# An inner seven-product scheme for one product of the SwiGLU up stage, from the third pair of column tiles on

## The chip, the cores and the metric

The kernel runs on one core of one Trainium2 chip. The metric is the device time of one execution in microseconds (us), the median of several runs; below, a time is that of the whole kernel unless a stage is named. The engines are TensorE (PE, with its weight loads shown apart as PEld), VectorE (DVE), ScalarE (ACT), GpSimd (POOL) and SyncE (SP, which here only issues DMAs).

## What is computed

One block of an encoder on a sequence of 1024 tokens with 1024 channels, in float32. The part that matters here is the last one: the norm and the SwiGLU feed-forward network with 2816 hidden columns.

```python
mod = (silu(c) @ w_ada + b_ada)
shift1, scale1, gate1, shift2, scale2, gate2 = split(mod, 6)
h = rms_norm(x, norm1_w) * (1 + scale1) + shift1
x = x + gate1 * hybrid_mixer(h, w_in, ..., w_out)   # gated DeltaNet heads beside a short gated conv
h = rms_norm(x, norm2_w) * (1 + scale2) + shift2
x = x + gate2 * ((silu(h @ w_gate) * (h @ w_up)) @ w_down)
return rms_norm(x, norm_f_w)
```

## The kernel before, in words

**Arithmetic.** Large products are made in a rounded float32 format (fp32r) from split operands: each operand is a high part (rounded, made by ACT) and a low part (the rest, made by DVE), and a product is three matmuls, high x high, high x low and low x high, added in one PSUM bank. A matmul has a 128 x 128 stationary operand and a moving one of 512 columns; a bank holds 128 x 512.

**Stages.** The conditioning vector and the w_in projection come first, then the two head groups, w_out, the norm, the up stage (gate and up) and the down stage. Until the w_out stage a planner sets the order of the instructions; its lines show as L448 in the profile. From the second half of w_out on, the order is written out by hand, and each engine's instructions show as L89 (PE) or L90 (the others), the lines of the helper that issues them.

**The w_out stage, second half.** `w_out_tile(t, ch)` is one tile of 128 tokens by 512 channels; `norm_tile` and `norm_stats` make the norm of a token tile (ACT sums the squares, POOL works on one column, DVE scales). `first_half` transposes the first four normed token tiles into operand tiles `H[k][0]` for eight groups k of 128 channels: k = 0 to 3 are the operand B11, k = 4 to 7 are B21. `tr_split` is four transposes into a bank, then the high part on ACT and the low part on DVE. `sums_x(i)` makes the operand sums of the outer scheme, in place; `early_load` and `early_mat` get the first weights ready.

**The up stage.** It runs over 11 pairs p = 0 to 10 of column tiles (256 of the 2816 hidden columns, for gate and up, q = 0 and 1). In each pair the two halves of the channels and the two halves of the tokens form a 2 x 2 block product, made with seven block products in place of eight (the scheme of Strassen and Winograd). The list `STEPS` names their order, the bank and the operands of each:

```python
STEPS = (("X", "A11", "B11", True), ("Y", "A12", "B21", True), ("X", "S2", "T2", False), ("Z", "S1", "T1", True),
         ("X", "S3", "T3", False), ("Z", "S4", "B22", False), ("X", "A22", "T4", False))
```

A operands are weights and their sums S1 to S4 (they change with each pair: class `Weights` with `load`, `sum_n`, `cast` for the high part on ACT, `low` on DVE). B operands are tokens and their sums T1 to T4; they are fixed, made once in pair 0. `run(p, s)` issues step s of pair p on PE: two q of four k of three matmuls, 24 in all, each of 512 columns. `block(p, s)` follows it and issues what the other engines do behind that step: `keep` (ACT copies a bank into SBUF), `close` (DVE adds a bank to such a copy), `silu`, `act` (the product of the gate and up halves), the weights of later steps, and DMA writes of finished results (`store`, issued by `flush` on SP). `block(p, 6)` makes the weights A12 of the next pair's step 1; `block(p, 0)` makes the sums S1 and S2 and the last product of the pair before, `c[o]["z5"][1]`. `slot` hands out the SBUF tiles for split weights from a ring of eight; `prep_load`, `prep_gate` and `prep_sums` make operand sums of w_down for the down stage. Pair 0 has an order of its own, since its steps wait for the fixed operands (`t_split` makes T2, T1, T3, T4 and B22 there, each with four banks of transposes).

The order of the instructions on each engine is the order in which the program issues them. A tile's pool and its tag decide which buffer it takes, and an instruction waits until the last user of that buffer is done.

Of the kernel before, what the change touches and what calls it, by code (L numbers as in the profile page):

```python
# [51 lines left out]
def kernel(  # L52
# [79 lines left out]
    def flat(ap):  # L132
        return ap.rearrange("p a b -> p (a b)")
# [69 lines left out]
    def h_slot(k, hf):  # L203
        return hp_.tile([P, 2, HT], F32R, name=nm(f"h{k}_{hf}"), tag=f"H{k}_{hf}")
# [337 lines left out]
    s2c = cst.tile([P, KB], F32, name="s2c", tag="s2c")  # L542
    b2c = cst.tile([P, KB], F32, name="b2c", tag="b2c")
    db2 = cst.tile([P, 4], F32, name="db2", tag="db2")
    su = []

    sim = Sim(seq, dict(pe=T_START[0], dve=T_START[1], act=T_START[2], pool=T_START[3], sp=T_START[4]))
# [952 lines left out]
    def pmm(o, l, r, s_, e_, more=False):  # L1500
        pe("pe", PE.matmul(o, l, r, start=s_, stop=e_, skip_group_check=more))
# [36 lines left out]
    def norm_tile(t):  # L1538
        keep_x2(t, (0,))
        norm_scale(t, norm_stats(t))  # L1540
# [25 lines left out]
    def first_half(ks):  # L1566
        for k in ks:
            H[k][0] = tr_split(lambda: h_slot(k, 0), [x2n[i][:, k * P:(k + 1) * P] for i in range(4)], allb.get("tr"), b2c[:, k:k + 1])

    def w_out_tile(t, ch):  # L1570
# [40 lines left out]
    first_half(range(4))  # L1611
    w_out_tile(5, 1)
    keep_x2(5, (1,))
    first_half(range(4, 8))
    early_load(0)
    early_load(1)
    sums_x(0)
    w_out_tile(5, 0)
    norm_tile(5)
    w_out_tile(6, 1)  # L1620
    keep_x2(6, (1,))
    sums_x(1)
    w_out_tile(6, 0)
    norm_tile(6)
    w_out_tile(7, 1)
    early_mat(0)
    norm_stats(7, 1)
    sums_x(2)
    early_mat(1)
# [13 lines left out]
    class Weights:  # L1643
# [53 lines left out]
        def mat(self, n):  # L1697
            for q in range(2):
                self.cast(n, q)
                self.low(n, q)  # L1700

    n_slot = [0]

    def slot():
        n_slot[0] += 1
        n = n_slot[0] - 14
        if n <= 0 or n % 8 in (5, 6, 7, 0):
            return hl_t([P, 2, 4, P])
        return mp.tile([P, 2, 4, P], F32R, name=nm("u"), tag="gl", bufs=4)
# [24 lines left out]
    def run(p, s, q_=(0, 1)):  # L1734
        b, an, bn, first = STEPS[s]
        if first and 0 in q_:
            for q in (0, 1):
                bk[p][q][b] = bank_tile(bk[p][q][b], "acc")
        for q in q_:
            u, ps = W[p].u[an][q], bk[p][q][b]  # L1740
            for k in range(4):
                x_ = B[bn][k]
                for n, (wi, xi) in enumerate(((0, 0), (0, 1), (1, 0))):
                    pmm(ps, u[:, wi, k, :], x_[:, xi, :], first and k == 0 and n == 0, k == 3 and n == 2, not first)

    def cc(p, n):
        if p == 0 and n == "p1":
# [27 lines left out]
    def store(p, n, t):  # L1775
        pend.append((am_scr[p, A_IX[n]], t))
# [28 lines left out]
    def block(p, s):  # L1805
        w, n = W.get(p), W.get(p + 1)
        last = p == NP - 1
        if s == 0:
            if p > 0:
                o = p - 1  # L1810
                ACT.activation(c[o]["z5"][1], bk[o][0]["X"], AF.Silu)
            if w:
                w.sum_n("S1")
                w.sum_n("S2")
                for q in (0, 1):
                    w.cast("S2", q)
            if p > 0:
                a12 = c[o]["z5"][1]
                DVE.tensor_tensor(a12, bk[o][1]["X"], a12, ALU.mult)
                store(o, "A12", a12)  # L1820
            if w:
                for q in (0, 1):
                    w.low("S2", q)
        elif s == 1:
            if w:
                keep(p, "p1", "X")
                w.cast("S1", 0)
                w.cast("S1", 1)
            if p > 0:
                o = p - 1  # L1830
                a11, s1, a21 = c[o]["p1"][0], c[o]["p1"][1], c[o]["u2"][0]
                DVE.tensor_tensor(a11, s1, a11, ALU.subtract)
                DVE.tensor_tensor(a21, c[o]["z5"][1], a11, ALU.subtract)
                store(o, "S2", a11)
                store(o, "S4", a21)
            if w:
                w.low("S1", 0)
                w.low("S1", 1)
                w.sum_n("S3")
        elif s == 2:  # L1840
            close(p, "p1", "Y")
            w.cast("S3", 0)
            silu(p, "p1")
            w.cast("S3", 1)
            w.low("S3", 0)
            w.low("S3", 1)
            act(p, "p1")
            store(p, "A11", c[p]["p1"][0])
            w.sum_n("S4")
        elif s == 3:  # L1850
            keep(p, "u2", "X")
            w.mat("S4")
            prep_gate(p - 1)
        elif s == 4:
            keep(p, "z5", "Z")
            w.mat("A22")
            prep_sums(p - 1)
            if last:
                first_mats(0, "A11", am_scr)
        elif s == 5:  # L1860
            close(p, "z5", "X")
            if n:
                n.cast("A11", 0)
            silu(p, "z5")
            if n:
                n.cast("A11", 1)
                n.low("A11", 0)
                n.low("A11", 1)
            act(p, "z5")
            store(p, "A22", c[p]["z5"][0])  # L1870
            if last:
                first_mats(1, "B11", None)
        elif s == 6:
            close(p, "u2", "Z")
            if n:
                n.cast("A12", 0)
            silu(p, "u2")
            if n:
                n.cast("A12", 1)
                n.low("A12", 0)  # L1880
                n.low("A12", 1)
            act(p, "u2")
            a11, a21, a22, s1, s3 = c[p]["p1"][0], c[p]["u2"][0], c[p]["z5"][0], c[p]["p1"][1], c[p]["u2"][1]
            DVE.tensor_tensor(s1, a21, a22, ALU.add)
            DVE.tensor_tensor(s3, a11, a21, ALU.subtract)
            store(p, "S1", s1)
            store(p, "S3", s3)
            if last:
                first_mats(2, "A12", am_scr)

# [80 lines left out]
    for p in range(1, NP):  # L1971
        for s in range(7):
            if s == 0:
                prep_load(p - 1)
            if s == 3 and p < NP - 1:
                W[p + 1] = Weights(p + 1)
                W[p + 1].load(0)
            if s == 5 and p < NP - 1:
                W[p + 1].load(1)
            if p == NP - 1 and s in (3, 5, 6):  # L1980
                first_load(*{3: (0, "A11"), 5: (1, "B11"), 6: (2, "A12")}[s])
            if s != 6:
# [217 lines left out]
```

## Time and profile before

| | us |
|---|---|
| median of 3 runs | 1166.29 (1165.78 to 1166.97) |
| profiled execution, its own time | 1166.65 |
| its span, first to last instruction | 1164.9 |
| PE busy | 1154.4 (99%) |
| DVE busy | 921.1 (79%) |
| ACT busy | 542.7 (47%) |
| POOL busy | 61.9 (5%) |

The granted TensorE clock is 0.999 of full speed. Busy time of an engine is the time that its own records cover. The records of PE are longer than their spacing, since matmuls are pipelined: what a matmul costs in a full queue is the distance between the starts of two of them, not the length of its record. In the timeline, a row is a run of like instructions with the start of the first and the length of all; the bracket at its end is the idle time of the engine ahead of it and what ended it.

### The profile page before, as it was taken

Reading aid. Unit: us, or ns where it says so; the run is one execution under the profiler, and the core shown is the slowest. Engines: PE = TensorE matmul, PEld = TensorE weight load, DVE = VectorE, ACT = ScalarE, POOL = GpSimd, SP = SyncE. Lnnn points to the kernel's source line nnn. Section 1 sums busy time; section 2 is a strip of 40 time slices with the busy share of each in tenths; the row PEclk is TensorE's granted clock in tenths of the full one; section 3 lists DMA queues with packets and bytes.
Section 4 is the critical chain, followed back from the end, with each engine's and each line's share of the span. In section 5 each row is a group of like instructions: output and inputs, shape, how many; then the busy total and the mean of one; then the engine's idle time right before and its main releaser. Section 6 shows DMA issues by size and latency. Waiting matters only on the chain.

```text
span 1164.9 us, 16388 instructions
## 1 busy us (share of the span) xinstructions
PE 1154.4 (99%) x5552; PEld 965.7 (83%) x5552; DVE 921.1 (79%) x1702; ACT 542.7 (47%) x1181; POOL 61.9 (5%) x100
## 2 busy tenths in 40 slices
PE   9999999999999999999999999999999999999997
PEld 7888888888888888888888888888888888888886
DVE  7899889899987898658776777776777687688676
ACT  6779633469634552326333333333333365443343
POOL 1110001002101010200000000000000000000002
PEclk9999999999999999999999999999999999999999
DMA  9823454534225455434164466445554589869403
GB/s 358 325 91 102 150 163 147 187 112 154 89 77 161 160 193 194 163 107 147 61 235 145 139 217 205 165 143 208 190 192 141 183 328 394 293 204 340 144 33 145
DMA packets 127540, 209.15 MB, mean 180 GB/s; under 512 B 20576, under 2 KB 45152, under 8 KB 127456
## 3 DMA queue, kind: packets, MB, share of 16 engines
q1 hardware_dynamic: 122080, 204.90, 51.3%
q10 hardware_dynamic: 5376, 3.21, 0.9%
q8 instruction: 44, 0.72, 0.2%
q14 instruction: 40, 0.33, 0.1%
HBM read 153.01 MB, written 55.05 MB: 179 GB/s over the span
## 4 chain that ended last, share of the span: by engine, by line
PE 94%; DVE 2%; DMA 2%; ACT 1%; issue 1%; SPq 0%; ACTq 0%; DVEq 0%
PE acc L89 35%; PE acc L448 25%; PE dn L89 17%; PE o L89 4%; PE o L448 4%; PE A L448 1%; PE K L448 1%; DMA wr<-in_w_in_dram 1%; DVE xo L90 1%; PE ab L448 1%; PE kk L448 1%; PE O L448 1%; PE u L448 1%; PE w L448 1%; DVE T L90 1%
## 5 line engine op out<-in xcount | busy, mean ns | idle before, releaser
L448 PE MATMUL acc<-h,u 128*128 128x512 f32 x1200 | 298.4, 397 | 0.0
L448 PEld LDWEIGHTS acc<-h,u 128*128 128x128 f32 x1200 | 219.4, 188 | 42.2 <-issue 0.5
L89 PE MATMUL acc<-h,hl 128*128 128x512 f32 x600 | 140.1, 390 | 0.0
L89 PEld LDWEIGHTS acc<-h,hl 128*128 128x128 f32 x600 | 112.4, 188 | 23.3
L89 PE MATMUL acc<-h,u 128*128 128x512 f32 x456 | 106.1, 389 | 0.0
L89 PE MATMUL acc<-T,hl 128*128 128x512 f32 x432 | 101.4, 390 | 0.1
L89 PEld LDWEIGHTS acc<-h,u 128*128 128x128 f32 x456 | 85.6, 188 | 17.8
L89 PEld LDWEIGHTS acc<-T,hl 128*128 128x128 f32 x432 | 80.9, 188 | 17.2 <-ACT cc L90 0.5
L90 DVE TENSOR_TENSOR xo<-xo,dn 128x512 f32<-128x512 f32 x84 | 57.1, 685 | 43.1 <-PE dn L89 35.8
L89 PE MATMUL dn<-h,h 128*128 128x512 f32 x396 | 90.7, 389 | 0.0
L90 ACT COPY cc<-acc 128x512 f32<-128x512 f32 x66 | 38.4, 590 | 108.4 <-PE acc L89 108.4
L89 PEld LDWEIGHTS dn<-h,h 128*128 128x128 f32 x396 | 74.3, 188 | 15.4
L89 PE MATMUL acc<-T,u 128*128 128x512 f32 x360 | 84.0, 389 | 0.0
L89 PEld LDWEIGHTS acc<-T,u 128*128 128x128 f32 x360 | 67.6, 188 | 14.0
L448 ACT CAST u<-raw 128x512 fp32r<-128x512 f32 x66 | 40.7, 621 | 63.7 <-PE acc L448 60.3
L90 DVE TENSOR_TENSOR cc<-cc,acc 128x512 f32<-128x512 f32 x66 | 43.9, 683 | 29.8 <-PE acc L89 29.8
L90 DVE TENSOR_TENSOR hl<-R,hl 128x512 fp32r<-128x512 f32 x60 | 39.5, 688 | 33.4 <-ACT hl L90 33.4
L448 DVE TENSOR_TENSOR u<-raw,u 128x512 fp32r<-128x512 f32 x82 | 56.1, 686 | 9.1 <-ACT u L448 8.9
L448 DVE SCALAR_TENSOR_TENSOR cv<-pr,cols_a,cv 128x512 f32<-128x512 f32 x72 | 53.4, 748 | 0.9 <-ACT cv L448 0.5
L90 ACT CAST h<-rw 128x512 fp32r<-128x512 f32 x57 | 32.7, 618 | 39.3 <-PE dn L89 34.6
L90 DVE TENSOR_TENSOR u<-R,u 128x512 fp32r<-128x512 f32 x46 | 30.1, 688 | 20.5 <-ACT u L90 20.5
L90 ACT CAST hl<-R 128x512 fp32r<-128x512 f32 x60 | 35.6, 622 | 23.1 <-DVE R L90 10.7
(349 smaller groups left out, 1988.2 us busy)
## 6 DMA issues: line engine op xcount, KB each, us to landing
raw<-in_w_in_dram SPq DMA_DIRECT2D x82, 256.0 KB, 3.2
am_scr<-cc SPq DMA_DIRECT2D x77, 256.0 KB, 4.5
raw<-in_w_ada_dram SPq DMA_DIRECT2D x56, 256.0 KB, 3.3
rw<-am_scr SPq DMA_DIRECT2D x55, 256.0 KB, 5.0
rw<-bm_scr SPq DMA_DIRECT2D x53, 256.0 KB, 5.1
bm_scr<-raw SPq DMA_DIRECT2D x51, 256.0 KB, 5.4
R<-in_w_gate_dram SPq DMA_DIRECT2D x22, 512.0 KB, 3.9
R<-in_w_up_dram SPq DMA_DIRECT2D x22, 512.0 KB, 5.2
```

Source lines behind the costliest of these rows:

```text
L89: return call(*a, **k)
L90: ins = call(*a, **k)
L448: ins = call(*a, **k)
```

## The change

In pairs p = 2 to 10, step 1 (A12 x B21 into the Y banks of gate and up) is made by a second, inner seven-product scheme. Its 2 x 2 blocks are: the gate and the up columns on one side, the two halves of the four channel groups (k = 4, 5 and k = 6, 7) on the inner side, and the two halves of the 512 tokens on the other. Each inner product m1 to m7 is two k of three matmuls with 256 columns. The Y bank of gate is used for the inner sums x, that of up for y and z (256 columns each):

- m1, m2, m5, m6 and m3 are issued in the place of step 1, m7 between the two q of step 2, m4 behind step 2. After m1, m5, m6 and m7 ACT copies the half bank into a tile `L`, before the next product is added to that half.
- `inner_sums`, `inner_cast` and `inner_low` take the place of the casts and lows of A12 in `block(p - 1, 6)`: four sums of 256 columns on DVE, and split weights for three sets of 512 and one of 256 columns in place of two of 512.
- `close_inner` takes the place of the closing of Y: two additions of 512 and three of 256 columns in place of two of 512.
- `keep(p, "p1", "X")` is issued ahead of the inner products, and the last product of the pair before ahead of the sums S1 and S2. The ring's count goes with 16 splits per pair in place of 14.
- The fixed operand B21 gets the inner sums q1, q2, q3 and a fourth one, which overwrites a half of H[4] and H[5]. `inner_half` makes their raw sums from the transposes' banks in the w_out stage (which makes the transposes in the order k = 4, 6, 5, 7), `inner_split` splits them there, in three calls at three places, and `inner_last` makes the fourth sum in pair 1, in two calls behind steps 2 and 3.
- A scratch area for DMA descriptors is set to a smaller size, which frees SBUF.

The diff, cut to its core:

```diff
+    def inner_half(a):
+        DVE.tensor_tensor(db3[:, a:a + 1], b2c[:, 6 + a:7 + a], b2c[:, 4 + a:5 + a], ALU.subtract)
+        bank = {}
+        for k in (4 + a, 6 + a):
+            bank[k] = allb.get("tr")
+            H[k][0] = tr_split(lambda: h_slot(k, 0), [x2n[i][:, k * P:(k + 1) * P] for i in range(4)], bank[k], b2c[:, k:k + 1])
+        pa, pb = bank[4 + a], bank[6 + a]
...
+        f1, f2, f3 = fq[a] = t[0][:, a, 0:HN], t[0][:, a, HN:HT], t[1][:, a]
+        DVE.tensor_copy(f3, pa[:, HN:HT])
+        DVE.tensor_tensor(f1, f3, pa[:, 0:HN], ALU.subtract)
+        DVE.tensor_tensor(f2, pb[:, HN:HT], f1, ALU.subtract)
+        DVE.tensor_tensor(f3, pb[:, HN:HT], f3, ALU.subtract)
+    def inner_split(i):
...
+                ACT.activation(hi, f, AF.Identity, bias=col, scale=1.0)
+                DVE.scalar_tensor_tensor(lo, f, col, hi.bitcast(F32), ALU.add, ALU.subtract)
+    def inner_last(a):
+        t = wst.tile([P, 2, HN], F32, name=nm("qt"), tag="aacc", bufs=1)
+        DVE.tensor_tensor(t, H[6 + a][0][:, :, 0:HN].bitcast(F32), tq["q2"][:, :, a, :].bitcast(F32), ALU.subtract)
+        DVE.tensor_tensor(t[:, 0], t[:, 0], t[:, 1], ALU.add)
+        q4 = H[4 + a][0][:, :, HN:HT]
+        split(t[:, 0], q4[:, 0], q4[:, 1], DVE, DVE)
...
-    first_half(range(4, 8))
+    inner_half(0)
+    inner_half(1)
     early_load(0)
     early_load(1)
     sums_x(0)
     w_out_tile(5, 0)
     norm_tile(5)
+    inner_split(0)
     w_out_tile(6, 1)
     keep_x2(6, (1,))
     sums_x(1)
     w_out_tile(6, 0)
     norm_tile(6)
+    inner_split(1)
     w_out_tile(7, 1)
     early_mat(0)
+    inner_split(2)
     norm_stats(7, 1)
...
+        def inner_sums(self):
+            g, u = self.m["A12"]
+            L = self.L = mp.tile([P, 4, 2, P], F32, name=nm("L"), tag="L", bufs=1)
+            DVE.tensor_tensor(L[:, 0], u[:, 0:2], u[:, 2:4], ALU.add)
+            DVE.tensor_tensor(L[:, 1], L[:, 0], g[:, 0:2], ALU.subtract)
+            DVE.tensor_tensor(L[:, 3], g[:, 0:2], u[:, 0:2], ALU.subtract)
+            DVE.tensor_tensor(L[:, 2], g[:, 2:4], L[:, 1], ALU.subtract)
...
-        n = n_slot[0] - 14
+        n = n_slot[0] - 12
...
+    INNER = {"m1": (0, 0, "x"), "m2": (0, 2, "y"), "m5": (1, 0, "z"), "m6": (1, 2, "x"), "m3": (2, 0, "z"), "m7": (2, 2, "x"), "m4": (3, 2, "x")}
...
+    def inner(p, ms):
...
+        for m in ms:
+            i, k0, d = INNER[m]
+            first = m in ("m1", "m2", "m5")
+            u = W[p].iu[i]
+            for k in range(2):
+                for n, (wi, xi) in enumerate(((0, 0), (0, 1), (1, 0))):
+                    pmm(iw[p][d], u[:, wi, k0 + k, :], inner_b(m, k, xi), first and k == 0 and n == 0, k == 1 and n == 2, not first)
+            if m in ("m1", "m5", "m6", "m7"):
...
+                ACT.copy(ik[p][:, {"m1": 0, "m6": 1, "m5": 2, "m7": 3}[m]], iw[p][d])
+    def close_inner(p, n):
+        (g, u), K, w = c[p][n], ik[p], iw[p]
+        DVE.tensor_tensor(g, g, flat(K[:, 0:2]), ALU.add)
+        DVE.tensor_tensor(u[:, HN:HT], u[:, HN:HT], K[:, 2], ALU.add)
+        DVE.tensor_tensor(g, g, w["yz"], ALU.add)
+        DVE.tensor_tensor(u[:, HN:HT], u[:, HN:HT], K[:, 3], ALU.add)
+        DVE.tensor_tensor(u[:, 0:HN], u[:, 0:HN], w["x"], ALU.add)
+    LATE = {2: lambda: inner_last(0), 3: lambda: inner_last(1)}
...
         if s == 0:
             if p > 0:
                 o = p - 1
-                ACT.activation(c[o]["z5"][1], bk[o][0]["X"], AF.Silu)
+                a12 = c[o]["z5"][1]
+                ACT.activation(a12, bk[o][0]["X"], AF.Silu)
+                DVE.tensor_tensor(a12, bk[o][1]["X"], a12, ALU.mult)
+                store(o, "A12", a12)
             if w:
                 w.sum_n("S1")
                 w.sum_n("S2")
...
-            close(p, "p1", "Y")
+            if p < 2:
+                close(p, "p1", "Y")
+            else:
+                close_inner(p, "p1")
...
         elif s == 6:
             close(p, "u2", "Z")
-            if n:
+            if n and p:
+                n.inner_sums()
+                n.inner_cast(0)
+            elif n:
                 n.cast("A12", 0)
             silu(p, "u2")
-            if n:
+            if n and p:
+                n.inner_cast(1)
+                n.inner_low(0)
+                n.inner_low(1)
+            elif n:
...
+            if n and p:
+                for i in (2, 3):
+                    n.inner_cast(i)
+                    n.inner_low(i)
...
-            run(p, s)
+            if s == 1 and p > 1:
+                keep(p, "p1", "X")
+                inner(p, ("m1", "m2", "m5", "m6", "m3"))
+            elif s == 2 and p > 1:
+                run(p, s, (0,))
+                inner(p, ("m7",))
+                run(p, s, (1,))
+                inner(p, ("m4",))
+            else:
+                run(p, s)
             block(p, s)
+            if p == 1 and s in LATE:
+                LATE[s]()
```

More of the change, by code (lines that the diff above doesn't have):

```diff
@@ L544 @@
     db2 = cst.tile([P, 4], F32, name="db2", tag="db2")
+    db3 = cst.tile([P, 2], F32, name="db3", tag="db3")
     su = []
@@ L1568, in first_half @@
             H[k][0] = tr_split(lambda: h_slot(k, 0), [x2n[i][:, k * P:(k + 1) * P] for i in range(4)], allb.get("tr"), b2c[:, k:k + 1])
+    HN = HT // 2
+    tq = {n: hp_.tile([P, 2, 2, HN], F32R, name=n, tag=n) for n in ("q1", "q2", "q3")}
+    fq = {}
+    def inner_half(a):
[5 more added lines that the diff above has]
+        pa, pb = bank[4 + a], bank[6 + a]
+        if not fq:
+            fq["t"] = gp.tile([P, 2, HT], F32, name="qf12", tag="A0", bufs=1), gp.tile([P, 2, HN], F32, name="qf3", tag="qs0", bufs=1)
+        t = fq["t"]
+        f1, f2, f3 = fq[a] = t[0][:, a, 0:HN], t[0][:, a, HN:HT], t[1][:, a]
[4 more added lines that the diff above has]
+    def inner_split(i):
+        for a in (0, 1):
+            f, q = fq[a][i], tq[f"q{i + 1}"]
+            hi, lo = q[:, 0, a, :], q[:, 1, a, :]
+            if i == 0:
+                split(f, hi, lo, DVE)
+            else:
+                col = (b2c[:, 6 + a:7 + a], db3[:, a:a + 1])[i - 1]
+                ACT.activation(hi, f, AF.Identity, bias=col, scale=1.0)
[6 more added lines that the diff above has]
+        split(t[:, 0], q4[:, 0], q4[:, 1], DVE, DVE)
     def w_out_tile(t, ch):
@@ L1700, in mat, with inner_cast, inner_low @@
                 self.low(n, q)
+        def inner_sums(self):
[5 more added lines that the diff above has]
+            DVE.tensor_tensor(L[:, 2], g[:, 2:4], L[:, 1], ALU.subtract)
+            Lf = L.rearrange("p s k c -> p (s k) c")
+            self.iu = [None] * 4
+            self.src = [g, Lf[:, 0:4], Lf[:, 4:8], u[:, 2:4]]
+        def inner_cast(self, i):
+            u = self.iu[i] = slot()
+            ACT.copy(u[:, 0] if i < 3 else u[:, 0, 2:4], self.src[i])
+        def inner_low(self, i):
+            u = self.iu[i]
+            hi, lo = (u[:, 0], u[:, 1]) if i < 3 else (u[:, 0, 2:4], u[:, 1, 2:4])
+            DVE.tensor_tensor(lo, self.src[i], hi.bitcast(F32), ALU.subtract)
     n_slot = [0]
@@ L1744, in run, with inner_b @@
                     pmm(ps, u[:, wi, k, :], x_[:, xi, :], first and k == 0 and n == 0, k == 3 and n == 2, not first)
+    iw, ik = {}, {}
+    INNER = {"m1": (0, 0, "x"), "m2": (0, 2, "y"), "m5": (1, 0, "z"), "m6": (1, 2, "x"), "m3": (2, 0, "z"), "m7": (2, 2, "x"), "m4": (3, 2, "x")}
+    def inner_b(m, k, xi):
+        if m in ("m1", "m4"):
+            return H[4 + k][0][:, xi, 0:HN] if m == "m1" else H[4 + k][0][:, xi, HN:HT]
+        if m in ("m2", "m3"):
+            return H[6 + k][0][:, xi, 0:HN] if m == "m2" else H[6 + k][0][:, xi, HN:HT]
+        return tq[{"m5": "q1", "m6": "q2", "m7": "q3"}[m]][:, xi, k, :]
+    def inner(p, ms):
+        if p not in iw:
+            x_, yz = bank_tile(bk[p][0]["Y"], "acc"), bank_tile(bk[p][1]["Y"], "acc")
+            iw[p] = dict(yz=yz, y=yz[:, 0:HN], z=yz[:, HN:HT], x=x_[:, 0:HN])
+        for m in ms:
[6 more added lines that the diff above has]
+            if m in ("m1", "m5", "m6", "m7"):
+                if p not in ik:
+                    ik[p] = mp.tile([P, 4, HN], F32, name=nm("L"), tag="L", bufs=1)
+                ACT.copy(ik[p][:, {"m1": 0, "m6": 1, "m5": 2, "m7": 3}[m]], iw[p][d])
[7 more added lines that the diff above has]
+    LATE = {2: lambda: inner_last(0), 3: lambda: inner_last(1)}
     def cc(p, n):
@@ L1816, in block @@
                     w.cast("S2", q)
[L1817 to L1820, printed above, removed]
             if w:
@@ L1825, in block @@
             if w:
-                keep(p, "p1", "X")
+                if p < 2:
+                    keep(p, "p1", "X")
                 w.cast("S1", 0)
@@ L1840, in block @@
         elif s == 2:
-            close(p, "p1", "Y")
+            if p < 2:
+                close(p, "p1", "Y")
+            else:
+                close_inner(p, "p1")
             w.cast("S3", 0)
@@ L1874, in block @@
             close(p, "u2", "Z")
-            if n:
+            if n and p:
+                n.inner_sums()
+                n.inner_cast(0)
+            elif n:
                 n.cast("A12", 0)
             silu(p, "u2")
-            if n:
+            if n and p:
[3 more added lines that the diff above has]
+            elif n:
                 n.cast("A12", 1)
+                n_slot[0] += 2
                 n.low("A12", 0)
@@ L1983 @@
                 flush()
-            run(p, s)
+            if s == 1 and p > 1:
+                keep(p, "p1", "X")
+                inner(p, ("m1", "m2", "m5", "m6", "m3"))
[4 more added lines that the diff above has]
+                inner(p, ("m4",))
+            else:
+                run(p, s)
             block(p, s)
+            if p == 1 and s in LATE:
+                LATE[s]()
     m_ctx.__exit__(None, None, None)
@@ L2186 @@
     from concourse.bass_utils import run_bass_kernel_spmd as _run
-    nc = _bacc.Bacc("TRN2", target_bir_lowering=False, num_devices=1)
+    nc = _bacc.Bacc("TRN2", target_bir_lowering=False, num_devices=1, dynamic_dma_scratch_size=1024)
     arrays, args = {}, []
```

## The prediction

> **What bounds the kernel now.** I read the profile page first, then its windows, the timeline of one pair, and the waits.
>
> ```profile
> span 1164.9 us, 16388 instructions
> PE 1154.4 (99%) x5552; PEld 965.7 (83%) x5552; DVE 921.1 (79%) x1702; ACT 542.7 (47%) x1181; POOL 61.9 (5%) x100
> PEclk9999999999999999999999999999999999999999
> ...
> PE 94%; DVE 2%; DMA 2%; ACT 1%; issue 1%; SPq 0%; ACTq 0%; DVEq 0%
> ```
>
> TensorE (PE) is busy for 99% of the span, at full granted clock in every slice, and is 94% of the chain that ended last. One pair of the up stage, from the windows (columns: length, then busy time and instructions of each engine):
>
> ```profile
> core 0: us, PE busy (x) PEld busy (x) DVE busy (x) ACT busy (x) POOL busy (x), PEclk, DMA share, GB/s
> 675.75:713.83 38.08, 38.08 (x170) 31.53 (x169) 27.33 (x40) 13.41 (x24) 0.00 (x0) 1.00 0.53 178
> ```
>
> PE has no gap in the 38.08 us; VectorE (DVE) has 10.75 us free and ScalarE (ACT) 24.67. The timeline of PE gives the steps (start, length):
>
> ```profile
> 681.78 5.60 PE L89 MATMUL acc<-h,hl 128*128 128x512 f32 x24
> 687.22 5.60 PE L89 MATMUL acc<-h,u 128*128 128x512 f32 x24
> 692.66 5.60 PE L89 MATMUL acc<-T,u 128*128 128x512 f32 x24
> ```
>
> A step starts every 5.44 us, so a 512-column matmul costs 5.44 / 24 = 0.2267 us, and 7 x 24 of them are the 38.08. The waits of the whole up stage behind pair 1 name only other engines as the waiting ones:
>
> ```profile
> ACT cc L90 <- PE acc L89: 127.7, 62, 3.6
> ...
> DVE hl L90 <- ACT hl L90: 33.2, 14, 3.0
> ...
> DVE cc L90 <- PE acc L89: 27.7, 17, 2.0
> ```
>
> So time is won here only by streaming less on PE, and lost only where PE is made to wait.
>
> **The change part by part.** *1. The products.* In each of the nine pairs p = 2 to 10, step 1 (A12 x B21) becomes seven products of 2 x 3 matmuls with 256 columns: 42 short for 24 long. Five stand in step 1's place, m7 and m4 inside step 2. PE's rows of pair 2, first before (acc_6177 and acc_6178 are the two Y banks, gate and up; h_0 is B21, then T_998 begins step 2):
>
> ```order
> L89 MATMUL acc_6177<-h_0_954_5185,hl_6117 128x512 x3
> L89 MATMUL acc_6177<-h_0_956_5193,hl_6117 128x512 x3
> L89 MATMUL acc_6177<-h_0_958_5201,hl_6117 128x512 x3
> L89 MATMUL acc_6177<-h_0_960_5209,hl_6117 128x512 x3
> L89 MATMUL acc_6178<-h_0_954_5185,hl_6120 128x512 x3
> L89 MATMUL acc_6178<-h_0_956_5193,hl_6120 128x512 x3
> L89 MATMUL acc_6178<-h_0_958_5201,hl_6120 128x512 x3
> L89 MATMUL acc_6178<-h_0_960_5209,hl_6120 128x512 x3
> L89 MATMUL acc_6138<-T_998_5473,hl_6169 128x512 x3
> ```
>
> The same place after it (acc_6229 and acc_6230 are the Y banks, u_ the inner weights, q_ the new operand sums):
>
> ```order
> L89 MATMUL acc_6229<-h_0_954_5190,u_6160 128x256 x3
> L89 MATMUL acc_6229<-h_0_958_5213,u_6160 128x256 x3
> L89 MATMUL acc_6230<-h_0_956_5198,u_6160 128x256 x3
> L89 MATMUL acc_6230<-h_0_960_5221,u_6160 128x256 x3
> L89 MATMUL acc_6230<-q_5054,u_6163 128x256 x6
> L89 MATMUL acc_6229<-q_5055,u_6163 128x256 x6
> L89 MATMUL acc_6230<-h_0_956_5198,u_6170 128x256 x3
> L89 MATMUL acc_6230<-h_0_960_5221,u_6170 128x256 x3
> L89 MATMUL acc_6187<-T_998_5501,hl_6219 128x512 x3
> ```
>
> These are m1, m2, m5 (q_5054), m6 (q_5055) and m3. m6 goes on in the bank half that m1 filled, m3 in the one that m5 filled, each with ACT's copy of the half in between; m7 and m4 (not shown) come behind step 2's two halves.
>
> What is a 256-column matmul worth? No fp32r one is in the trace of before; these are the nearest rows, from the timelines and the groups by form:
>
> ```profile
> 12.83 1.06 PE L448 MATMUL heat<-ident,ones 128*128 128x128 f32 x8
> ...
> L448 PE MATMUL heat<-ident,ones 128*128 128x128 f32 x40 | 5.0, 275 | 0.0
> L448 PEld LDWEIGHTS heat<-ident,ones 128*128 128x128 f32 x40 | 4.8, 192 | 0.0
> 528.33 1.91 PE L89 MATMUL tr<-ident,raw 128*128 128x128 f32 x16
> 62.20 1.02 PE L448 MATMUL RS<-raw,ones 128*128 128x512 f32 x2
> L448 PE MATMUL RS<-raw,ones 128*128 128x512 f32 x2 | 1.0, 592 | 0.0
> ```
>
> Eight f32 matmuls, each with its own weight load (x40 loads for x40 matmuls), stand (1.06 - 0.275) / 7 = 0.112 us apart; sixteen transposes (1.91 - 0.275) / 15 = 0.109. A pair of f32 matmuls with 512 columns stands 1.02 - 0.592 = 0.428 apart, so 128 such columns stream for about 0.107: the load beside them costs no more than 0.005. Lower bound for the short matmul: 0.112, the shortest spacing with a load each. In proportion to columns: 0.2267 / 2 = 0.1134. Upper bound with hidden loads: taking the slope of those f32 rows, 0.428 / 2 / 512 us per column, 512 columns stream in 0.214 and 0.013 is a fixed part, so 0.107 + 0.013 = 0.120. I take 0.114, near proportion, as the transposes' 0.109 shows hardly a fixed part. Per pair that saves 5.44 - 42 x 0.114 = 0.65 us; for nine pairs **-5.9** (-6.6 at 0.112, -3.6 at 0.120).
>
> The Trainium skill ("TensorE: Matmul & The Clock Gate", Back-to-back issue gap) lists 262 cycles for 256 columns and 518 for 512, which is a constant 6 cycles per matmul; an estimate from that page, 262/518 of 0.2267 = 0.1147, would make the saving 5.6 us.
>
> *2. The wait of m3.* m3 must not write before ACT has copied m5, and only m6 (six short matmuls) stands between.
>
> ```profile
> 687.42 0.59 ACT L90 COPY cc<-acc 128x512 f32<-128x512 f32 x1 [2.13 <-PE acc L89]
> ...
> L90 ACT COPY cc<-acc 128x512 f32<-128x512 f32 x66 | 38.4, 590 | 108.4 <-PE acc L89 108.4
> L448 ACT ACTIVATE jk<-kT 128x128 bf16<-128x128 f32 x32 | 9.0, 282 | 2.0 <-DVE nq L448 1.5 <-DVE kt L448 0.4
> ...
> 550.44 0.60 ACT L90 COPY cc<-acc 128x512 f32<-128x512 f32 x1
> ...
> 551.09 0.76 PEld L89 LDWEIGHTS acc<-T,hl 128*128 128x128 f32 x4 [0.51 <-ACT cc L90]
> ```
>
> ACT starts 0.20 us after PE has gone on to the next step (687.22 to 687.42). A copy of 256 columns lies between 0.282 (128) and 0.590 (512): 0.38 on the line through both. The weight load starts 0.05 after ACT's end (551.04 to 551.09) and takes 0.11. In all 0.74, against 6 x 0.114 = 0.68 of m6: PE waits 0.06 per pair, **+0.5** for nine. Bounds: nothing if m6 streams at 0.120 and ACT is 0.02 faster; 0.25 a pair (+2.3) if the copy costs nearly that of 512 columns.
>
> *3. DVE and ACT inside the pair.* ACT's rows of pair 2 ahead of step 2, before (acc_6138 and acc_6139 are the X banks):
>
> ```order
> L90 ACTIVATE cc_6031<-acc_5850 128x512
> L90 CAST hl_6169<-S_6167 128x512
> L90 CAST hl_6171<-S_6167 128x512
> L90 COPY cc_6203<-acc_6138 128x512
> L90 COPY cc_6203<-acc_6139 128x512
> L90 CAST u_6206<-S_6165 128x512
> L90 CAST u_6208<-S_6165 128x512
> ```
>
> and after (acc_6187 and acc_6188 are X, L_6237 takes the copies of the inner products):
>
> ```order
> L90 ACTIVATE cc_6069<-acc_5878 128x512
> L90 CAST hl_6219<-S_6217 128x512
> L90 CAST hl_6221<-S_6217 128x512
> L90 COPY cc_6226<-acc_6187 128x512
> L90 COPY cc_6226<-acc_6188 128x512
> L90 COPY L_6237<-acc_6229 128x256
> L90 COPY L_6237<-acc_6230 128x256
> L90 COPY L_6237<-acc_6229 128x256
> L90 CAST hl_6265<-S_6215 128x512
> L90 CAST hl_6267<-S_6215 128x512
> L90 COPY L_6237<-acc_6229 128x256
> ```
>
> The copies that release PE now queue behind ACT's casts of S2, which wait for DVE's sums. The rows there, and a 256-column DVE operation:
>
> ```profile
> 681.53 1.23 DVE L90 TENSOR_TENSOR S<-S,R 128x1024 f32<-128x1024 f32 x1
> ...
> 682.85 1.14 ACT L90 CAST u<-S 128x512 fp32r<-128x512 f32 x2 [2.99 <-DVE S L90]
> 684.70 0.59 ACT L90 COPY cc<-acc 128x512 f32<-128x512 f32 x1 [0.71 <-PE acc L89]
> ...
> L448 DVE TENSOR_TENSOR L<-L,ct 128x256 f32<-128x256 f32 x8 | 3.4, 421 | 0.9 <-DMA dl<-L 0.8
> 535.64 2.48 DVE L90 TENSOR_TENSOR h<-tr,h 128x512 fp32r<-128x512 f32 x4
> ```
>
> In a queue a 512-column operation costs (2.48 - 0.68) / 3 = 0.60, with 0.09 overlapped; 256 columns so 0.34 (0.42 without overlap). Ahead of the sums DVE gets four inner sums (1.36), lows of one 512 and one 256 more (0.94), and the moved A12 product (0.60): 2.9 us. The sums, done at 682.76, come at 685.7, the casts end at 686.9, both keep copies by about 688.0 (the second may start at 687.4). m1's copy can start when m1 is done plus 0.20, at 687.22 + 0.68 + 0.20 = 688.1, and m6 needs it at 687.22 + 18 x 0.114 = 689.27, less 0.16 for the load and 0.38 for the copy: 688.7. A margin of 0.6 us: **0**. With 0.42 for each of the five short ones, 0.4 of that margin is gone. Busy time rises by 3.3 on DVE (to 30.6 of 37.4 us) with the 1.02 of the inner closing, and by 2.5 on ACT; both fit. The added operations issue no DMA, and the DMA and GpSimd queues keep their order.
>
> *4. The operand sums ahead.* They add 14 short DVE operations and six short ACT ones in the w_out stage, whose DVE rows are:
>
> ```profile
> 501.38 1.28 DVE L90 SCALAR_TENSOR_TENSOR x<-x,st,u 128x1024 f32<-128x1024 f32 x1 [2.62 <-POOL st L90]
> ...
> 509.20 0.69 DVE L90 TENSOR_TENSOR x<-x,o 128x512 f32<-128x512 f32 x1 [2.35 <-PE o L89]
> ...
> 514.77 0.69 DVE L90 TENSOR_TENSOR x<-x,o 128x512 f32<-128x512 f32 x1 [0.99 <-PE o L89]
> ...
> 522.86 1.28 DVE L90 SCALAR_TENSOR_TENSOR h<-x,st,u 128x1024 f32<-128x1024 f32 x1 [1.85 <-POOL st L90]
> ```
>
> The eight of the first part (2 x 4 x 0.34 and two of one column, about 3.1) and the first split (0.7) are taken up by the waits for PE, 2.35 the largest; the second split (0.7) by the 0.99. The third has no wait for PE behind it: the 1.85 ahead of 522.86 waits for statistics of the row that is itself late. So pair 0's DVE work is 0.7 to 0.8 late. There:
>
> ```profile
> 537.36 0.49 PE L89 MATMUL tr<-ident,x 128*128 128x128 f32 x3
> ...
> 538.67 0.49 PE L89 MATMUL tr<-ident,x 128*128 128x128 f32 x3
> ```
>
> The fourth group of these transposes starts 0.55 us after DVE's row of 535.64 has ended (538.12), which frees its bank. 0.8 less 0.55 shows at once, and more later in pair 0: **+0.5** (0 to 0.9). The last sums (one of 512, three of 256: 1.7 us each) stand in pair 1 at two places where DVE waits for ACT anyway:
>
> ```profile
> 585.20 1.29 DVE L90 TENSOR_TENSOR hl<-R,hl 128x512 fp32r<-128x512 f32 x2 [1.86 <-ACT hl L90]
> ...
> 590.64 1.29 DVE L90 TENSOR_TENSOR u<-R,u 128x512 fp32r<-128x512 f32 x2 [1.74 <-ACT u L90]
> ```
>
> Cover 1.86 and 1.74: **0**; without it up to +3.4, once.
>
> Sum: -5.9 + 0.5 + 0.5 = -4.9 against the profiled execution's 1166.65 us (span 1164.9 and 1.75 around it), which lies 0.36 above the median of the runs, 1166.29. From that median: 1161.4.
>
> **The rivals.** *A, a fixed part in each matmul* (0.120): -3.6 + 0.2 (m6 then covers nearly all of the copy) + 0.5 = -2.9, 1163.4. For it: 0.2267 is more than twice 0.107. Against: the 0.109.
>
> *B, PE waits in each pair for ACT's copies*, because DVE's sums are late by more than the margin of 0.6. Half a microsecond of stall each: -4.9 + 4.5, 1165.9; a whole one 1170.4. For it: all the new copies stand in one queue behind casts that depend on DVE. Against: nearly 7 us of DVE's time stay free in the pair.
>
> *C, slower: the weight load is not hidden.* A short stream of 0.113 has no room to spare over a load of 0.112; if load and stream took turns, a short matmul would cost 0.225, 42 of them 9.45, +4.0 a pair, +36 in nine: 1203. Half hidden, 0.169: +1.7 a pair, about 1182. It decides from 5.44 / 42 = 0.130 on, where nothing is saved. Against: the f32 rows at 0.112, where load and stream are as long as here and hardly add. The Trainium skill (same page, Part 3, What overlaps and what doesn't) has a load overlap with running matmuls only where the row groups differ; here all are 128 rows, which is this rival. The trace disagrees with that rule for f32, and shows no fp32r matmul as short.
>
> *D, the operand sums are not covered* in pair 1: -4.9 + 3.4, 1164.8.
>
> **How the numbers follow.** Forecast 0.58, A 0.13, B 0.12, C 0.10, D 0.07. Forecast and A are faster by over 0.2% (2.3 us, about what a measurement of this kernel can tell from no change), with a little of B and D: 0.70. Within 0.2% (1164.0 to 1168.6): most of B and D, 0.14. Slower: C, the end of B, and what I do not see, 0.16. The range starts at 1159.0 (0.112 and neither wait give -6.6, 1159.7; 0.109 would give 1158.5) and reaches through A and D to B with half a microsecond: 1166.3.
>
> **What would show it.** Right: step 1 of pairs 2 to 10 at 3.4 to 3.5 us for 30 short matmuls (0.114), pairs 37.4 to 37.6 us long, one wait of PE or its loads on ACT of some 0.06 ahead of m3, none ahead of m6, and a gap of about half a microsecond in pair 0. Wrong: short matmuls above 0.125 apart, or pairs of over 38 us with PE idle for ACT's copies.

## The result and the profile after

The changed kernel takes 1164.21 us (median of 17 runs, 1163.49 to 1164.82) against 1166.43 us for the kernel before in the same runs: a ratio of 0.9982, 95% interval 0.9975 to 0.9989. It is faster by 2.2 us, where 4.9 were forecast. Its profiled execution takes 1164.59 us, 2.06 less than the one before. Its span is 2.4 us shorter, 1162.5 against 1164.9; the time outside the span has grown by 0.34, from 1.75 to 2.09.

From the profile page of the changed kernel:

```profile
span 1162.5 us, 16907 instructions
...
PE 1152.4 (99%) x5714; PEld 971.4 (84%) x5714; DVE 959.1 (83%) x1807; ACT 563.1 (48%) x1241; POOL 60.1 (5%) x100
...
PE 93%; DVE 3%; ACT 2%; DMA 1%; issue 1%; SPq 0%; POOL 0%; ACTq 0%; DVEq 0%; POOLq 0%
```

PE is the bound as before, with 162 more matmuls (nine pairs of 18) and 2.0 us less of busy time. One inner pair, that is, one of the pairs 2 to 10, from the windows (columns as in the prediction):

```profile
649.58:687.30 37.72, 37.72 (x187) 32.08 (x186) 30.55 (x50) 15.43 (x31) 0.00 (x0) 1.00 0.54 181
```

PE has no gap in it. A pair lasts 37.72 us in place of 38.08 (from the starts of the single instructions, 37.726): 0.354 saved, where 0.59 were forecast (0.65 less the wait of m3). In a pair, DVE's busy time rises by 3.2 us (3.3 forecast) and ACT's by 2.0 (2.5 forecast). The timeline of PE shows the changed steps of such a pair:

```profile
687.30 1.60 PE L89 MATMUL acc<-h,u 128*128 128x256 f32 x12
688.74 1.60 PE L89 MATMUL acc<-q,u 128*128 128x256 f32 x12
690.17 0.88 PE L89 MATMUL acc<-h,u 128*128 128x256 f32 x6
690.89 2.90 PE L89 MATMUL acc<-T,hl 128*128 128x512 f32 x12
693.63 0.88 PE L89 MATMUL acc<-q,u 128*128 128x256 f32 x6
694.34 2.91 PE L89 MATMUL acc<-T,hl 128*128 128x512 f32 x12
697.09 0.88 PE L89 MATMUL acc<-h,u 128*128 128x256 f32 x6
```

and, in the pair ahead of it, step 3 and the start of step 4:

```profile
660.08 5.63 PE L89 MATMUL acc<-h,hl 128*128 128x512 f32 x24
665.54 5.60 PE L89 MATMUL acc<-T,u 128*128 128x512 f32 x24
```

The 30 short matmuls in step 1's place take 690.89 - 687.30 = 3.59 us, 0.1197 each. The forecast was 0.114, and the rival with a fixed part in each matmul said 0.120. No wait stands in the pair; m3 follows m6 at 690.17 with a pause of 0.01. With m7 and m4, of 0.71 each, the 42 short ones take 5.02 us (from the single instructions). But the long matmuls behind the short ones are slower than before: twelve of them take 2.74 and 2.75 us in step 2 (2.72 before), and step 3 takes 665.54 - 660.08 = 5.46 (5.44 before; 5.467 from the single instructions). That is 0.07 a pair. So a pair saves 5.44 - 5.02 - 0.07 = 0.35.

The other change is in pair 0. PE around step 4 of pair 0 (the one that is added to the X banks after ACT has copied them), first before:

```profile
548.03 2.98 PE L89 MATMUL acc<-h,hl 128*128 128x512 f32 x12
551.09 5.73 PE L89 MATMUL acc<-T,hl 128*128 128x512 f32 x24
```

and after:

```profile
548.38 2.98 PE L89 MATMUL acc<-h,hl 128*128 128x512 f32 x12
551.85 5.76 PE L89 MATMUL acc<-T,hl 128*128 128x512 f32 x24 [0.50 <-ACT cc L90]
```

The step stands 3.06 us behind the rows above it before, 3.47 after: 0.41 more of waiting, and some 0.1 more in the transposes ahead of it. What it waits for are ACT's copies of the X banks, and ACT is as late as DVE, whose low parts of T2 begin 0.77 later. DVE's and ACT's rows before:

```profile
529.69 2.73 DVE L90 SCALAR_TENSOR_TENSOR T<-tr,b2c,T 128x512 fp32r<-128x512 f32 x4 [1.56 <-ACT T L90]
...
550.44 2.06 ACT L90 COPY cc<-acc 128x512 f32<-128x512 f32 x4
```

and after:

```profile
530.46 2.73 DVE L90 SCALAR_TENSOR_TENSOR T<-tr,b2c,T 128x512 fp32r<-128x512 f32 x4 [1.27 <-ACT T L90]
...
551.20 2.06 ACT L90 COPY cc<-acc 128x512 f32<-128x512 f32 x4
```

Of these 0.77, 0.29 stand ahead of pair 0 for PE too, which leaves 0.48. Call the stretch the distance from the last transpose of the first group in pair 0 to the first matmul of the down stage. Read from the trace's single instructions it is 418.37 us before and 415.69 after: -2.68 = 9 x 0.354 saved (3.18) less 0.50 in pair 0. Ahead of the stretch the two traces differ by 0.29 us, which arises in the first 16 us; behind it, by nothing. So the span is 2.4 us shorter, and 0.34 more outside the span leave the 2.06 of the profiled execution. The 0.34 are no accident of one execution: over the 17 runs of the changed kernel the time outside the span is 2.14 us on average, in those of the kernel before that are on record with the experiments it lies between 1.73 and 1.90. With the inner scheme from pair 6 on it is 1.78 again, so the new operations alone do not explain it, and no run shows what sets it.

### The profile page after: what moved, and what is told of

The parts are those of the page before. It is cut to its first block, busy times and chain, and to the rows that moved or that the text cites. A ratio compares the mean times of both kernels' runs of the same rounds, so it can differ in the third digit from the quotient of the medians.

```text
span 1162.5 us, 16907 instructions
## 1 busy us (share of the span) xinstructions
PE 1152.4 (99%) x5714; PEld 971.4 (84%) x5714; DVE 959.1 (83%) x1807; ACT 563.1 (48%) x1241; POOL 60.1 (5%) x100
## 4 chain that ended last, share of the span: by engine, by line
PE 93%; DVE 3%; ACT 2%; DMA 1%; issue 1%; SPq 0%; POOL 0%; ACTq 0%; DVEq 0%; POOLq 0%
PE acc L89 34%; PE acc L448 25%; PE dn L89 17%; PE o L448 4%; PE o L89 3%; PE A L448 1%; PE K L448 1%; DVE xo L90 1%; PE ab L448 1%; PE O L448 1%; PE kk L448 1%; DVE T L90 0%; PE qk L448 0%; DVE hl L90 0%; DMA raw<-in_w_ada_dram 0%
## 5 line engine op out<-in xcount | busy, mean ns | idle before, releaser
L448 PE MATMUL acc<-h,u 128*128 128x512 f32 x1200 | 298.6, 398 | 0.0
L89 PE MATMUL acc<-T,hl 128*128 128x512 f32 x552 | 131.3, 391 | 0.5 <-ACT cc L90 0.5
L89 PEld LDWEIGHTS acc<-T,hl 128*128 128x128 f32 x552 | 102.3, 188 | 21.2 <-ACT cc L90 0.9
L89 PE MATMUL acc<-h,u 128*128 128x512 f32 (+1 forms) x480 | 91.8, 341 | 0.0
L89 PE MATMUL acc<-T,u 128*128 128x512 f32 x240 | 56.0, 390 | 0.0
L90 ACT CAST hl<-S 128x512 fp32r<-128x512 f32 x44 | 25.3, 622 | 61.3 <-DVE S L90 61.3
L89 PEld LDWEIGHTS acc<-T,u 128*128 128x128 f32 x240 | 45.1, 188 | 9.3
L90 ACT ACTIVATE cc<-cc 128x512 f32<-128x512 f32 x33 | 20.9, 632 | 64.2 <-DVE cc L90 63.8
L90 ACT CAST u<-R 128x512 fp32r<-128x512 f32 (+1 forms) x60 | 34.1, 584 | 34.3 <-DVE R L90 34.2
L90 DVE TENSOR_TENSOR hl<-S,hl 128x512 fp32r<-128x512 f32 x44 | 28.5, 688 | 26.9 <-ACT hl L90 26.9
```

What stands on the lines that cost most here:

```text
L89: return call(*a, **k)
L90: ins = call(*a, **k)
L448: ins = call(*a, **k)
```

## The experiments

**The width of a matmul.** The kernel before is taken and its step 1 is cut into pieces of fewer columns.

```diff
+        if s == 1 and p in CUT:
+            ...
+                for cn in cuts:
+                    for k in range(4):
+                        for n, (wi, xi) in enumerate(((0, 0), (0, 1), (1, 0))):
+                            pmm(ps[:, c0:c0 + cn], u[:, wi, k, :], B[bn][k][:, xi, c0:c0 + cn], ...)
+                    c0 += cn
```

> The kernel before, with step 1 of pairs 2 to 9 cut into pieces of fewer columns (2 x 256, 384 + 128, 320 + 192, 448 + 64, 2 x 256 with the same weights one behind the other, 4 x 128 and 8 x 64, 240 + 272 and 248 + 264), and in pair 9 two rows of 12 extra matmuls of 256 columns with stationary operands of 64 and of 32 columns, which are overwritten. Read from the trace is the distance between matmuls of one width. Theory 1, a fixed part of 0.013 us in every matmul beside 0.417 ns a column (from 0.2267 at 512 and 0.1197 at 256): 0.200 at 448, 0.173 at 384, 0.147 at 320, 0.093 at 192, 0.067 at 128; the same weights twice and the narrower stationary operands change nothing, 0.120. Theory 2, time in proportion to columns (0.443 ns each) with a floor of 0.120 from the weight load: 0.198 at 448, 0.170 at 384, 0.142 at 320, 0.120 at 192, 128 and 64; with a stationary operand of 64 columns 0.1134 at 256 columns.

The timeline of its PE, in windows that hold one width each (a row counts the matmuls of its window; spacing is the length less one record, over the count less one; a record is 0.28 us at 256 columns, 0.34 at 384, 0.27 at 192 and below):

```profile
610.37 5.92 PE L89 MATMUL acc<-h,hl 128*128 128x256 f32 x48
...
648.96 1.92 PE L89 MATMUL acc<-h,u 128*128 128x384 f32 x10
...
690.18 1.28 PE L89 MATMUL acc<-h,u 128*128 128x192 f32 x10
...
806.13 5.07 PE L89 MATMUL acc<-h,u 128*128 128x128 f32 x44
...
901.12 1.30 PE L89 MATMUL acc<-h,hl 128*64 128x256 f32 x10
```

Forty-eight matmuls of 256 columns, which do the work of step 1 undivided, stand 0.120 apart and take 5.75 us in place of 5.44. At 384 columns it is 0.174 to 0.176 (Theory 1 said 0.173, Theory 2 0.170); from the single instructions, 0.147 at 320 and 0.202 at 448. So from 256 columns up the spacing lies above proportion and near to Theory 1, a fixed part of about 0.013. Below, that theory fails: 192 and 128 columns stay at 0.11 (0.093 and 0.067 were expected), which is the floor of Theory 2, though at 0.111 and not at 0.120. And with a stationary operand of 64 columns the 256-column matmul takes (1.30 - 0.28) / 9 = 0.113, as only Theory 2 said. Neither holds as a whole. The rows of 256 columns with the same weights one behind the other took 0.120 as well.

**What the fixed part is.** The same with alternating widths and more widths of the stationary operand. (The whole times of the two ladders, 1192.79 and 1176.27 us in one run each, hold extra and narrower matmuls and are not used.)

> The kernel before, with step 1 cut in other ways: pair 2 alternates 512 columns (up) with 256 (gate), 12 of each, then 12 of 256; pair 3 one of 512 and two of 256; pair 4 alternates 256 columns of two banks; pair 5 has extra rows of 12 with stationary operands of 96, 112 and 64 columns (256 moving) and of 64 columns (512 moving), which are overwritten; pair 6 alternates 512 and 384; pair 7 has 288, 224, 416 and 96. Theory 1, the fixed part of 0.013 belongs to every matmul: 512 + 256 take 0.346, 512 + 256 + 256 take 0.466, two banks change nothing, and narrower stationary operands give 0.120. Theory 3, part of the fixed 0.013 is a 128-column weight load that a short stream does not hide entirely: the spacing at 256 grows from 0.1134 at 64 columns through 96 and 112 to 0.120 at 128, 512 columns stay at 0.2267 with 64, and a 256 behind a 512 takes 0.113, so that 512 + 256 take 0.340.

Groups by form in the windows of pair 5, and the timeline of pairs 2 and 4:

```profile
L89 PE MATMUL acc<-h,hl 128*112 128x256 f32 x12 | 1.5, 276 | 0.0
```

```profile
611.06 4.39 PE L89 MATMUL acc<-h,hl 128*128 128x512 f32 x24
...
687.67 5.80 PE L89 MATMUL acc<-h,u 128*128 128x256 f32 x47
```

With 112 or 64 stationary columns a 256-column matmul stands 0.1134 from the next (from the single instructions), with 128 columns 0.120. So with a narrower stationary operand it takes half of a long matmul's 0.2267, and 0.0064 more with one of 128 columns. That is the main point of Theory 3, but the spacing does not grow with the width as it said: 112 columns are as good as 64, and 96 lie higher, between 0.112 and 0.120. That the 0.0064 are a weight load which is not quite hidden is a reading and not shown: a narrower stationary operand also fills fewer rows of the PSUM bank, and no run separates the two. A 512-column matmul gains nothing from 64 stationary columns (0.229). The last part of Theory 3 is not borne out: alternating 512 and 256 columns, twelve of each, takes 4.39 less the last record of 0.28 and plus its spacing of 0.12, 4.23 us, 0.3525 a couple, more than the sum 0.3465 of the two by themselves. By the single instructions it is the long ones that are slower there, 0.236 on average, as the long ones behind the short are in the changed kernel; so putting short matmuls between long ones gains nothing. Two banks in turn (687.67) change nothing. Why 240 columns take 0.1115 and 256 take 0.120, from the single instructions of the first ladder, and why a long matmul is slower next to a short one, is left open.

**The inner scheme from pair 6 on.** The same code with the bound 2 replaced by 6; pairs 2 to 5 multiply an operand of which `inner_last` has already overwritten a part.

```diff
-            if s == 1 and p > 1:
+            if s == 1 and p >= PMIN:   # 6, and so at each place
```

> The changed kernel with the inner scheme from pair 6 on (five pairs in place of nine); the operand sums ahead are all there. Theory, a saving of 0.36 us in each inner pair less 0.5 us once: -1.3 us against the kernel before, about 1165.1, and pairs 2 to 5 of 38.08 us, 6 to 10 of 37.72. Rival, that part of the saving is lost elsewhere in the up stage by a cost in each pair that the trace puts on no wait: the pairs would not be of these lengths.

It took 1165.4 us, a ratio of 0.9994 (0.9985 to 1.0003), which by itself cannot be told from no change. The traces tell more: the stretch from pair 0 to the down stage is 417.09 us, 1.28 shorter than before, and 5 x 0.354 - 0.50 is 1.27. Pair 6 goes from 759.18 to 796.91 in PE's timeline:

```profile
759.18 5.60 PE L89 MATMUL acc<-h,hl 128*128 128x512 f32 x24
764.62 1.60 PE L89 MATMUL acc<-h,u 128*128 128x256 f32 x12
...
796.91 3.34 PE L89 MATMUL acc<-h,hl 128*128 128x512 f32 x14
```

That is 37.73 us; the saving is one per pair and nothing is lost elsewhere in the stretch.

**The margin of the copies.** Copies of X are repeated on ACT ahead of the inner products.

```diff
                 keep(p, "p1", "X")
+                for _ in range(1):     # 3 in the second kernel
+                    ACT.copy(c[p]["p1"][1], bk[p][1]["X"])
                 inner(p, ("m1", "m2", "m5", "m6", "m3"))
```

> The changed kernel with one more ACT copy of 512 columns (0.5 us, a copy repeated) ahead of the copies of the inner products, in every inner pair. Theory, m6 has a margin of 0.6 to 0.7 us for its copy: no wait of PE ahead of m6, pairs of 37.72 us, 1164.2. Rival, the copies are already the limit: 0.5 us more in each pair, 1168.7.

> The same with three more copies (1.5 us). Theory, the margin of 0.6 to 0.7 is used up and PE waits 0.7 to 0.9 ahead of m6 in every inner pair: nine times 0.8, 1171.4, slower than the kernel before by 5 us. Rival, ACT's queue has more room than thought: under 1166.

With one more copy the time was 1163.89 us (one run), the stretch from pair 0 to the down stage 415.70, and no row of PE's waits names the tile `L`. With three it was 1172.28 us, a ratio of 1.0058 (1.0045 to 1.0072). PE's waits and its timeline in the first inner pair of that kernel:

```profile
PE acc L89 <- ACT L L90: 5.9, 9, 0.7
```

```profile
613.61 0.88 PE L89 MATMUL acc<-q,u 128*128 128x256 f32 x6
615.15 0.98 PE L89 MATMUL acc<-q,u 128*128 128x256 f32 x6 [0.66 <-ACT L L90]
```

Nine waits, one in each inner pair, between m5 and m6, where the prediction had put them. The stretch is 424.00 us, 8.3 more than with none: 0.92 a pair (0.7 to 0.9 expected). ACT's rows in an inner pair, first in the changed kernel, then in this one:

```profile
686.98 1.11 ACT L90 COPY cc<-acc 128x512 f32<-128x512 f32 x2
688.27 0.37 ACT L90 COPY L<-acc 128x256 f32<-128x256 f32 x1 [0.18 <-PE acc L89]
```

```profile
611.86 2.96 ACT L90 COPY cc<-acc 128x512 f32<-128x512 f32 x5
```

The three copies add 2.96 - 1.11 = 1.85 us to ACT's queue, more than the 1.5 that the expectation put, and 0.92 of it reach PE, so 0.93 were to spare. About 0.2 to 0.3 of that is idle time of ACT ahead of m1's copy (0.18 by the row), and the rest, 0.6 to 0.7, is the margin of m6, as worked out.

**Pair 0, with GpSimd.** The low part of the third sum is taken from DVE.

```diff
+                if i == 2:
+                    POOL.tensor_scalar(f, f, col, None, ALU.add)
+                    POOL.tensor_tensor(lo, f, hi.bitcast(F32), ALU.subtract)
```

> The changed kernel, with the low part of the third operand sum (inner_split(2), two DVE operations of 256 columns) made on GpSimd. Theory: these 0.8 us of DVE are what makes pair 0 late by 0.5 us, so PE's wait at step 2 of pair 0 goes back from 0.76 to about 0.3 against the kernel before, and the time falls by about 0.5 us, to 1163.7. Rival, the lateness comes from inner_half earlier in the stage: no change, 1164.2; or GpSimd is so slow that the norm's statistics are late: some us more.

It took 1164.51 us (0.9987, 0.9979 to 0.9996), no better. GpSimd and then DVE in its timeline:

```profile
517.19 0.74 POOL L90 TENSOR_TENSOR q<-qf,q 128x256 fp32r<-128x256 f32 x1
517.91 1.89 POOL L90 TENSOR_SCALAR qf<-qf,db 128x256 f32<-128x256 f32 x1
```

```profile
517.21 1.26 DVE L90 TENSOR_TENSOR raw<-x,x 128x512 f32<-128x512 f32 x1
...
530.61 2.73 DVE L90 SCALAR_TENSOR_TENSOR T<-tr,b2c,T 128x512 fp32r<-128x512 f32 x4 [1.27 <-ACT T L90]
```

and the row of the changed kernel for the same DVE operation:

```profile
518.38 0.69 DVE L90 TENSOR_TENSOR raw<-x,x 128x512 f32<-128x512 f32 x1
```

While GpSimd works, the same DVE operation takes 1.26 in place of 0.69. DVE comes out of the stage not earlier but later: its row of T2 starts 0.93 us behind the last transpose of the first group (530.61 to 529.68), against 0.20 in the changed kernel (530.46 to 530.26). The stretch is 416.39 us, 0.70 longer than there. So the run does not separate the two theories, since more came back than was taken from DVE.

**Pair 0, with the splits elsewhere.** The high parts are made on ACT earlier, the low parts on DVE inside the norm, where DVE waits for GpSimd.

```diff
...
+    inner_hi(1)
+    inner_hi(2)
     w_out_tile(6, 0)
-    norm_tile(6)
-    inner_split(1)
+    norm_tile_with(6, (1, 2))   # norm_stats, then inner_lo(1), inner_lo(2), then norm_scale
     w_out_tile(7, 1)
     early_mat(0)
-    inner_split(2)
```

> The changed kernel with the splits of the operand sums placed elsewhere in the w_out stage: the high parts on ACT ahead of w_out_tile(5, 0) and w_out_tile(6, 0), the low parts on DVE between the norm's statistics and its scaling, where DVE waits 2.6 us for GpSimd. Theory, pair 0's wait comes from DVE being 1.0 us late at the end of the stage: DVE is then as early as in the kernel before, PE's gap at step 2 of pair 0 is 0.25 us again in place of 0.66, and the time falls by 0.5 us to about 1163.7. Rival, the lateness comes from the eight operations of inner_half: the gap stays, 1164.2.

It took 1163.36 us, a ratio of 0.9979 (0.9970 to 0.9988) to the kernel before: the best of all, though the interval overlaps that of the changed kernel. DVE's timeline at that place, and PE's at step 4 of pair 0:

```profile
510.00 0.88 DVE L90 SCALAR_TENSOR_TENSOR q<-qf,db,q 128x256 fp32r<-128x256 f32 x2
511.90 1.28 DVE L90 SCALAR_TENSOR_TENSOR x<-x,st,u 128x1024 f32<-128x1024 f32 x1 [1.02 <-POOL st L90]
```

```profile
547.35 2.98 PE L89 MATMUL acc<-h,hl 128*128 128x512 f32 x12
550.50 2.79 PE L89 MATMUL acc<-T,hl 128*128 128x512 f32 x11 [0.17 <-ACT cc L90]
```

The step follows 3.15 us behind the row above it (3.06 before, 3.47 in the changed kernel), and the stretch to the down stage is 415.20 us, 0.49 less than in the changed kernel and 9 x 0.354 less than before. So the place of the splits cost these 0.5 us, and `inner_half` costs next to nothing. (The expectations call this step 2 of pair 0; it is step 4.)

**The scratch area alone.**

> The kernel before with only the smaller scratch area for DMA descriptors. Theory: no change of the time (within 0.05%); the 0.3 us by which PE's first instructions start later in the changed kernel's trace are then the scatter of a start. Rival: the smaller area makes DMAs wait, and those 0.3 us show here too.

It took 1166.37 us (1.0002, 0.9993 to 1.001), and the stretch is 418.38 us: no change. The first matmul of the first projection starts at 15.65 us there, 15.57 before, 15.88 after and between 14.99 and 15.70 in the other runs, so the 0.3 us at the start are scatter.

## Why the prediction was wrong

*What held.* PE is the bound and waits for nothing inside the pairs; the direction was right. Pair 0 was forecast to lose 0.5 us and lost 0.50, for the reason given, splits that make DVE late: the experiment that moves them gives 0.49 of it back. The place was given only in part: 0.09 and not 0.25 show at the fourth group of transposes, and 0.41 at step 4, of which the prediction said no more than "later in pair 0". The last operand sums in pair 1 cost nothing: pair 1 of the changed kernel has the 38.08 us of the one before. The margin of 0.6 us for m6 was right, as the repeated copies show.

*What failed* is, first of all, one term of the sum, the price of the short matmul. I took 0.114 from the transposes' 0.109 and from proportion, and it is 0.1197 in a row and 5.02 / 42 = 0.1195 over a pair. So the 42 take 5.02 us where 4.79 were put, 0.23 more per pair and 2.05 in nine, and the saving falls from 5.9 to 3.8. The row of the transposes was the wrong neighbour. Matmuls of 192 and 128 columns show a floor of 0.111 with stationary operands of 128 columns, and the transposes stand at that floor (0.109 to 0.112), so nothing of a fixed part could be seen in them. They were read as a stream of 0.107 with 0.002 to 0.005 on top. (That the load of 128 columns sets this floor is likely but not shown. The lower bound of 0.112, called the shortest spacing with a load each, lay above the transposes' own 0.109; nothing hung on it.)

A second term was put at nothing without a reason: that the long matmuls of steps 2 and 3 cost what they did. Behind short ones they take 0.07 more in each pair, 0.6 in nine, so that 3.2 of the 3.8 are left. Third, the time outside the span was taken to stay at 1.75 us and grew by 0.34, so that the 2.68 of the stretch became 2.2 in the measured time, up to the scatter of the start.

The wait of m3, put at 0.06 a pair, is 0.01: with the slower m6 (0.72) the copy is nearly covered, as rival A had it. That makes up for most of the slower long matmuls, by luck.

The upper bound of the same paragraph, 0.120, was the value, and rival A, given 0.13, had the right price. It said 2.9 us less, and the stretch is 2.68 shorter. Its reason did not come: a fixed part in each matmul would have stayed with narrower stationary operands, where the spacing was 0.1134.

Rival C may have had the right suspicion with far too high a price: if the 0.0064 that a stationary operand of 128 columns costs are a weight load that is not hidden, that is all of it that shows, and not 0.11. The Trainium skill ("TensorE: Matmul & The Clock Gate", Back-to-back issue gap) says that in a stream the spacing is set by load and matmul together; the runs agree, with 0.1134 at 112 stationary columns and 0.120 at 128. Its rule that a load overlaps only where the row groups differ (Part 3, What overlaps and what doesn't) does not hold here: all loads used all 128 rows, and going from 112 to 128 stationary columns added 0.0064 to 0.1134, where a load and a stream that took turns would have come to 0.225 by the sum of rival C.

## What to carry to other kernels

Price a narrower matmul by a run of that width with the same stationary operand, or else by the bound that has the whole fixed part in it: here halving the columns cost 0.31 us on 5.44, nearly half of the 0.68 that seven products in place of eight take away. Look at the long matmuls behind the short ones as well, which cost 0.07 a pair here. A row at another width may sit on a floor and then tells nothing of the slope. And work that is to be hidden belongs into a wait that another engine sets, as DVE's 2.6 us for the norm's statistics, not behind it: moving three pairs of operations there was worth 0.49 us, beside 3.18 from all the inner products.

## What the runs showed of the hardware

In the ladder the granted clock fell while 96 matmuls of 64 columns ran in a row (pair 7, right behind 48 of 128 columns), which it does in the up stage of no other run here. Windows of that kernel, with the clock in the column PEclk:

```profile
805.85:811.15 5.30, 5.30 (x49) 5.30 (x48) 2.43 (x3) 2.25 (x4) 0.00 (x0) 1.00 0.10 36
811.15:828.00 16.85, 16.85 (x99) 16.85 (x98) 0.69 (x1) 1.14 (x2) 0.00 (x0) 0.62 0.00 0
828.00:835.00 7.00, 7.00 (x23) 5.62 (x23) 3.63 (x5) 0.59 (x1) 0.00 (x0) 0.70 0.54 162
```

Their spacing went from 0.112 to 0.213, although PE has no gap there, and the clock was still at 0.70 on average in the 7 us of long matmuls behind them. That the row of short matmuls is the cause is the reading; no second run tried it. And while GpSimd ran 256-column operations, a DVE operation beside them took 1.26 us in place of 0.69.
